# A planner's cost table with other figures for TensorE's products and GpSimd's powers (two-layer encoder, one core)

## The chip, the core and the metric

The kernel runs on one core of one Trainium2 chip. Five engines take part, each with its own instruction queue, which it works off in order: TensorE (PE; its weight loads are listed apart as PEld), ScalarE (ACT), VectorE (DVE), GpSimd (POOL) and SyncE (SP), which in this kernel issues every DMA. An instruction that waits for another engine holds up everything behind it in its own queue. The metric is the device time of one execution in microseconds (us); the time of a kernel is the median of its runs.

## The reference

The reference computes two layers of an encoder over one sequence of 256 tokens with 1024 features, all in float32. Each layer has an attention sublayer and a feed-forward sublayer:

```python
def mixer_sublayer(x, ...):
    proj = rms_norm(x, n1) @ w_in_l                      # 1024 -> 2560
    qa, ka, va, qd, kd, vd, qc, kc, vc = jnp.split(proj, cuts, axis=-1)
    out_a = neighbourhood_attention(...)                 # 4 heads, with a bias table
    out_d = dilated_window_attention(...)                # 6 heads, partial rotary
    out_c = gqa_block_attention(...)                     # 6 query heads on 2 key heads, axial rotary
    mix = jnp.concatenate([rms_norm(out_a, ...), rms_norm(out_d, ...), rms_norm(out_c, ...)], axis=-1)
    return x + mix @ w_out_l                             # 1024 -> 1024

def channel_sublayer(x, n2, w_gu, cw, cb, w_dn):
    g, u = jnp.split(rms_norm(x, n2) @ w_gu, 2, axis=-1) # 1024 -> 2 x 2816
    g = depthwise_conv_centred(g, cw, cb)                # three taps along the sequence
    return x + (jax.nn.gelu(g, approximate=False) * u) @ w_dn
```

Queries and keys are normed per head ahead of the scores.

## The kernel before

**Products.** A float32 product is made of three: each operand is split into a rounded high part and the rest, and `mm3` adds high × high, high × low and low × high into one PSUM bank. Weights come from HBM in units of up to 1 MB, into a ring of four raw buffers. ACT copies each unit into its high part (`wp_hi`), DVE subtracts to get the low part (`wp_lo`), in pieces of 512 columns; there are two buffers of each. Activations that are multiplied are transposed on TensorE, and ACT and DVE write high and low part (`act_hT`, `act_mixT_hi`, `act_mixT_lo`, `act_ch`, `act_cl`). PSUM has eight banks: four for accumulations of the projections (`psa_a`) and four for everything else (`psw_w`: scores, transposes, weighed values, the feed-forward's first products).

**Stages of a layer.** First come the input projections, in seven column groups (`projections`). The attention of 16 heads follows as a chain: scores on TensorE, maximum and exponential on DVE and ACT (`softens`), transposes on TensorE (`turn`), weighing with the values on TensorE (`weigh`), norm per group (`group_rstd`: squares on POOL, sums through products with ones on TensorE, a power on POOL). Between the steps of this chain the recording code puts filler: the rest of the projections and four of the six blocks of the output projection (class `Weave`; it counts the filler with a constant of its own, 2.4 columns per ns, which does not change). Then come the last two output blocks; `split_T(halves(0))` and `split_T(halves(1))`, which transpose the two halves of the new x into `act_hT`; and `mean_squares`, whose power on POOL gives `small_rx`. I call this place the feed-forward's head. The feed-forward part runs over 11 steps: a gate and an up block (`half_up`: per 128 rows of depth one product of 512 columns, high weight times high and low activations side by side, and one of 256, low weight times high), the convolution, the GELU, and a down block (`down`, products of 512 columns).

**The neighbourhood's bias table.** For each layer POOL copies a small table (`act_nab<-act_few`), SP writes it to HBM and reads it back along the diagonals (`na_repeat`, `na_diagonals`), and POOL adds a mask to it in three instructions (`act_nab<-act_nab,const_na`).

**Order of the work.** Nothing is issued while it is recorded. `Plan.add` notes each of the 5,580 operations with what it must wait for, and with a time from `cost()`. Then `Plan.order` simulates the five engines: again and again it takes, among all operations whose inputs are made, the one that can start first by its own clock; where two can start at the same time, the lower rank goes first. The rank is the place in the recording, plus a shift that the `later()` blocks give (weight splits 50, transposes of weights of attention 100, mixing 100, preparation of heads 30). A handover between engines costs a fixed time from a table (`HANDOVER`, for example 197 ns from TensorE to ACT); a buffer goes to its next user 170 ns after the last use. `Plan.emit` then issues the operations in that order, so the table decides on the order in each queue, and on the buffers, but not on what is computed. Since one line (345) issues everything, the profile shows one line for all instructions, and one reads it by the tiles' names.

In the simulation the start of an operation is

```python
at = max(o.at, free[e])      # inputs made, engine free; then the buffer's time
if at is not None and (best is None or (at, o.rank) < best[:2]):
    best = (at, o.rank, i)
```

Of the kernel before, what the change touches and what calls it, by code (L numbers as in the profile page):

```python
# [12 lines left out]
F32R = mybir.dt.float32r  # L13
# [202 lines left out]
class Plan:  # L216
# [15 lines left out]
    def add(self, engine, method, args, kw):  # L232
# [11 lines left out]
        if method == "matmul" and not kw["start"]:  # L244
            ins.append(args[0])
        o.ns, o.size = cost(engine.name, method, args, kw, ins)
        o.before, o.after, o.first, o.tiles = set(), [], [], []
        for v in ins + outs:
# [99 lines left out]
def cost(engine, method, args, kw, ins):  # L348

    out = args[0]  # L350
    if method == "dma_start":
        w = out if isinstance(out, View) else args[1]
        small = min(out.shape[-1], args[1].shape[-1]) < 128
        return 50, 4 * math.prod(w.shape) * (2 if small else 1)
    n = out.width()
    psum = any(v.tile.pool.psum for v in ins)
    if engine == "PE":
        if method == "transpose":
            return 110, 0
        n = args[2].width()  # L360
        if args[1].dtype == F32:
            return 108, 0
        return n / (2.4 if args[1].dtype == F32R else 1.2) + 2.5, 0
    if engine == "ACT":
        extra = 93 * sum(isinstance(kw.get(k), View) for k in ("scale", "bias")) + 90 * ("accum_out" in kw)
        return 0.833 * n + (47 if psum else 94) + extra, 0
    if engine == "DVE":
        if method in ("reduce_sum", "reduce_max"):
            n = args[1].width()
        per = 1.04  # L370
        if method in ("tensor_copy", "tensor_scalar_mul") and not psum:
            per = 0.52
        if method == "tensor_tensor_reduce":
            per = 1.3
        return per * n + (130 if method == "scalar_tensor_tensor" or method == "tensor_scalar_mul" and n > 16 else 70), 0
    if method == "memset":
        return 40 + 0.9 * n, 0
    if method == "tensor_copy":
        return 3.4 * n, 0
    if kw.get("op") == ALU.pow:  # L380
        return 300 + 165 * n, 0
    return 2.2 * n + 160, 0


# [958 lines left out]
```

## Time and profile before

| what | value |
| --- | --- |
| runs of the kernel | 631.75, 631.51, 630.89 us; median 631.51 |
| the profiled execution | 632.02 us |
| its span (first to last instruction) | 630.2 us |
| granted TensorE clock | 1.00 |
| TensorE busy | 616.0 us, 98% of the span |
| VectorE, ScalarE, GpSimd busy | 499.0 us (79%), 436.4 (69%), 90.6 (14%) |
| HBM traffic | 102.5 MB read, 1.5 MB written, 165 GB/s over the span |

The profile is taken from one execution. In its tables a row names the engine, the operation, and the tiles as output<-inputs; "x64" is a count. In a timeline the first two columns are start and duration in us, and brackets at the end hold the idle time of the engine before the row and what released it. The ends of products are modelled: the next product usually starts before the listed end of the one before, so the pace is read from starts, or from the length of a gapless run divided by its count. Layer 0's attention lies at about 16 to 128 us, its feed-forward part at 131 to 321; layer 1's attention at 322 to 436, and its feed-forward part at 438 to 626.

### The profile page before, as it was taken

To read this page: it belongs to the slowest core of one execution; us is meant where nothing else is said; L and a number is where in the kernel's file an instruction comes from. 1 tells how busy PE (TensorE), PEld (TensorE's weight loads), DVE (VectorE), ACT (ScalarE), POOL (GpSimd) and SP (SyncE) were. 2 spreads that over 40 slices of the span, in tenths; PEclk is the share of its full clock that TensorE was granted. 3 is DMA by queue.
4 is the path that set the end of the run, shared out by engine and by line. 5 is a ranking of instruction groups with operands and counts; after the bars stand their busy time and mean duration, and the time that the engine had idled before them with its cause. 6 is when DMAs were issued, how large, how long until landed. Compare 5 with 4: busy or idle time off the path is not lost.

```text
span 630.2 us, 9713 instructions
## 1 busy us (share of the span) xinstructions
PE 616.0 (98%) x3400; PEld 534.0 (85%) x3400; DVE 499.0 (79%) x1038; ACT 436.4 (69%) x1076; POOL 90.6 (14%) x139
## 2 busy tenths in 40 slices
PE   8998999999999999999999999999999999999997
PEld 6997888877888888888899989787888888888885
DVE  4799989899777777777877898988887777777775
ACT  6787998786665556556678989888756655666551
POOL 5755231350000000000013210311000000000000
PEclk9999999999999999999999999999999999999999
DMA  7894313486555655565434732134556555555511
GB/s 247 284 275 133 125 43 101 133 213 206 192 201 200 200 180 176 181 200 185 148 111 162 248 101 84 35 118 153 201 200 201 195 174 174 194 200 185 172 44 67
DMA packets 81408, 104.65 MB, mean 166 GB/s; under 512 B 9528, under 2 KB 69016, under 8 KB 81360
## 3 DMA queue, kind: packets, MB, share of 16 engines
q1 hardware_dynamic: 81360, 104.04, 51.1%
q8 instruction: 26, 0.43, 0.3%
q14 instruction: 22, 0.18, 0.1%
HBM read 102.54 MB, written 1.49 MB: 165 GB/s over the span
## 4 chain that ended last, share of the span: by engine, by line
PE 90%; DVE 5%; ACT 2%; POOL 1%; issue 1%; DMA 1%; SPq 0%; ACTq 0%; POOLq 0%
PE psw_w L345 48%; PE psa_a L345 41%; DVE wp_lo L345 1%; ACT act_s2k L345 1%; DVE act_s2k L345 1%; DVE act_z L345 1%; POOL small_rstd L345 1%; DMA const_x<-in_x_dram 1%; ACT wp_hi L345 1%; DVE small_mx L345 0%; ACT act_hT L345 0%; DVE small_ss L345 0%; DVE act_hT L345 0%; DVE act_cl L345 0%; SPq L345 0%
## 5 line engine op out<-in xcount | busy, mean ns | idle before, releaser
L345 DVE TENSOR_TENSOR wp_lo<-wp_raw,wp_hi 128x512 fp32r<-128x512 f32 (+2 forms) x348 | 250.7, 749 | 50.6 <-ACT wp_hi L345 48.8
L345 PE MATMUL psw_w<-act_hT,wp_hi 128*128 128x512 f32 x704 | 248.4, 394 | 3.6 <-DVE act_hT L345 3.6
L345 ACT CAST wp_hi<-wp_raw 128x512 fp32r<-128x512 f32 (+2 forms) x348 | 212.8, 659 | 26.9 <-PE psw_w L345 15.6
L345 PE MATMUL psw_w<-act_hT,wp_lo 128*128 128x256 f32 x704 | 198.3, 283 | 0.0
L345 PEld LDWEIGHTS psw_w<-act_hT,wp_hi 128*128 128x128 f32 x704 | 131.9, 188 | 34.6 <-DVE act_hT L345 4.7
L345 PEld LDWEIGHTS psw_w<-act_hT,wp_lo 128*128 128x128 f32 x704 | 132.3, 188 | 1.2
L345 PE MATMUL psa_a<-wp_hi,act_hT 128*128 128x384 f32 (+2 forms) x448 | 114.4, 335 | 0.0
L345 ACT COPY act_s2k<-psw_w 128x256 f32<-128x256 f32 x88 | 32.4, 372 | 81.4 <-PE psw_w L345 81.4
L345 PEld LDWEIGHTS psa_a<-wp_hi,act_hT 128*128 128x128 f32 x448 | 79.0, 189 | 2.5 <-DVE act_hT L345 0.2
L345 PE MATMUL psa_a<-wp_lo,act_hT 128*128 128x384 f32 (+2 forms) x224 | 75.2, 336 | 0.5 <-DVE wp_lo L345 0.5
L345 PE MATMUL psa_a<-wp_hi,act_ch 128*128 128x512 f32 x176 | 69.6, 395 | 0.2 <-ACT act_ch L345 0.2
L345 PE MATMUL psa_a<-wp_lo,act_ch 128*128 128x512 f32 x176 | 69.5, 395 | 0.0
L345 PE MATMUL psa_a<-wp_hi,act_cl 128*128 128x512 f32 x176 | 66.2, 395 | 0.3 <-DVE act_cl L345 0.3
L345 DVE TENSOR_TENSOR act_s2k<-psw_w,act_s2k 128x256 f32<-128x256 f32 x88 | 36.9, 423 | 31.2 <-ACT act_s2k L345 30.5
L345 PEld LDWEIGHTS psa_a<-wp_lo,act_hT 128*128 128x128 f32 x224 | 42.5, 190 | 3.2 <-DVE wp_lo L345 1.8
L345 PEld LDWEIGHTS psa_a<-wp_hi,act_cl 128*128 128x128 f32 x176 | 33.2, 188 | 8.5 <-DVE act_cl L345 0.8
L345 PEld LDWEIGHTS psa_a<-wp_hi,act_ch 128*128 128x128 f32 x176 | 33.1, 188 | 8.2 <-ACT act_ch L345 0.6
L345 PEld LDWEIGHTS psa_a<-wp_lo,act_ch 128*128 128x128 f32 x176 | 33.2, 189 | 6.8
L345 DVE SCALAR_TENSOR_TENSOR act_s2k<-act_s2k,act_cw,act_s2k 128x255 f32<-128x255 f32 x88 | 36.8, 480 | 1.4 <-ACT act_s2k L345 1.3
L345 ACT ACTIVATE act_s2k<-act_s2k,act_cw 128x256 f32<-128x256 f32 x44 | 24.1, 595 | 14.0 <-DVE act_s2k L345 14.0
L345 POOL TENSOR_TENSOR small_rstd<-small_ms,const_mh 128x6 f32<-128x6 f32 (+2 forms) x26 | 31.3, 1202 | 2.2
L345 POOL TENSOR_TENSOR small_s1x<-small_ssx 128x2 f32<-128x2 f32 x4 | 2.3, 582 | 200.5 <-ACT act_s2k L345 200.5
(112 smaller groups left out, 830.9 us busy)
## 6 DMA issues: line engine op xcount, KB each, us to landing
wp_raw<-in_w_gate_up_dram SPq DMA_DIRECT2D x44, 1024.0 KB, 5.1
wp_raw<-in_w_down_dram SPq DMA_DIRECT2D x22, 1024.0 KB, 4.8
wp_raw<-in_w_in_dram SPq DMA_DIRECT2D x14, 768.0 KB, 5.5
wp_raw<-in_w_in_dram SPq DMA_DIRECT2D x8, 1024.0 KB, 6.1
wp_raw<-in_w_out_dram SPq DMA_DIRECT2D x8, 768.0 KB
wp_raw<-in_w_out_dram SPq DMA_DIRECT2D x4, 512.0 KB, 3.8
act_nab<-dram_scr SPq DMA_DIRECT2D x4, 448.0 KB, 6.7
const_x<-in_x_dram SPq DMA_DIRECT2D x8, 128.0 KB, 3.6
```

The costliest lines, as they stand in the source:

```text
L345: getattr(o.engine.real, o.method)(*map(real, o.args), **{k: real(v) for k, v in o.kw.items()})
```

## The change

Two figures of `cost()` change. For a float32r product of n columns the time in the table was n/2.4 + 2.5 ns and is now 0.4405 n + 6.5 ns: for 512, 384 and 256 columns 215.8, 162.5 and 109.2 ns become 232.0, 175.7 and 119.3. The bfloat16 products that warm TensorE up at the start, 256 columns wide, go from 215.8 to 210 ns. A power on POOL of n columns goes from 300 + 165 n to 380 + 165 n ns. Transposes and the float32 products with ones keep their figures (110 and 108 ns).

```diff
@@ -360,7 +360,7 @@
         n = args[2].width()
         if args[1].dtype == F32:
             return 108, 0
-        return n / (2.4 if args[1].dtype == F32R else 1.2) + 2.5, 0
+        return (0.4405 * n + 6.5 if args[1].dtype == F32R else 210), 0
     if engine == "ACT":
         extra = 93 * sum(isinstance(kw.get(k), View) for k in ("scale", "bias")) + 90 * ("accum_out" in kw)
         return 0.833 * n + (47 if psum else 94) + extra, 0
@@ -378,7 +378,7 @@
     if method == "tensor_copy":
         return 3.4 * n, 0
     if kw.get("op") == ALU.pow:
-        return 300 + 165 * n, 0
+        return 380 + 165 * n, 0
     return 2.2 * n + 160, 0
```

The operations are the same 5,580 with the same operands; each engine gets them in another order, and some take another buffer of the same ring.

## The prediction

> **What bounds the kernel now.** I read the page's first lines first, then the table of busy time by stretch, the list of what TensorE waited for, and the timeline at each wait.
>
> ```profile
> span 630.2 us, 9713 instructions
> PE 616.0 (98%) x3400; PEld 534.0 (85%) x3400; DVE 499.0 (79%) x1038; ACT 436.4 (69%) x1076; POOL 90.6 (14%) x139
> PE 90%; DVE 5%; ACT 2%; POOL 1%; issue 1%; DMA 1%; SPq 0%; ACTq 0%; POOLq 0%
> ```
>
> TensorE is busy for 98% of the span and carries 90% of the chain that ended last. The change leaves its instructions as they are, so what can be won or lost is TensorE's idle time. Where it lies, by stretch (columns: stretch, its length, then busy time and count of PE, PEld, DVE, ACT, POOL, the granted clock, DMA):
>
> ```profile
> 24.00:32.00 8.00, 7.46 (x44) 6.67 (x43) 7.24 (x16) 5.79 (x32) 7.49 (x10) 1.00 0.67 226
> 48.00:60.00 12.00, 10.33 (x72) 9.31 (x71) 11.94 (x34) 9.30 (x34) 8.13 (x11) 1.00 0.41 131
> 85.00:92.00 7.00, 6.58 (x43) 5.61 (x42) 6.63 (x19) 6.13 (x19) 4.55 (x6) 1.00 0.13 48
> 120.00:130.00 10.00, 9.32 (x54) 7.60 (x53) 8.63 (x16) 6.06 (x14) 2.15 (x3) 1.00 0.49 150
> 130.00:140.00 10.00, 8.80 (x52) 7.28 (x51) 9.75 (x17) 8.45 (x22) 5.78 (x6) 1.00 1.19 269
> 150.00:155.00 5.00, 4.44 (x20) 3.15 (x19) 4.99 (x9) 3.61 (x9) 0.00 (x0) 1.00 0.36 108
> 155.00:300.00 145.00, 145.00 (x763) 123.98 (x762) 108.28 (x184) 86.39 (x157) 0.00 (x0) 1.00 0.57 191
> 390.00:400.00 10.00, 9.08 (x60) 7.76 (x60) 8.21 (x22) 9.11 (x28) 4.54 (x5) 1.00 0.18 53
> 436.00:447.00 11.00, 8.63 (x54) 7.29 (x53) 9.61 (x19) 8.61 (x23) 1.85 (x3) 1.00 0.36 113
> ```
>
> TensorE idles 0.54 us in 24–32, 1.67 in 48–60, and in the six later stretches 0.42, 0.68, 1.20, 0.56, 0.92 and 2.37, together 6.15. The feed-forward part (155–300) has none. The waits, summed over the run (us, times, longest):
>
> ```profile
> PE psw_w L345 <- DVE act_hT L345: 3.6, 4, 1.2
> PE psw_w L345 <- DVE act_cl L345: 1.3, 2, 0.9
> PE psw_w L345 <- POOL const_warm L345: 1.0, 1, 1.0
> PE psw_w L345 <- DMA const_x<-in_x_dram: 0.9, 1, 0.9
> ...
> PE psa_a L345 <- ACT act_ch L345: 0.2, 1, 0.2
> ```
>
> The 11 rows of this list add up to 10.2 us in 15 waits. The largest is act_hT, the normed input of the feed-forward part, at its head in both layers.
>
> **The change, part by part.** Two lines of the table change: the pace of a product and the time of a power.
>
> ```profile
> 157.59 11.22 PE psw_w L345 x64
> 168.81 5.58 PE psa_a L345 x24
> L345 POOL TENSOR_TENSOR small_rstd<-small_ms,const_mh 128x6 f32<-128x6 f32 x12 | 17.3, 1444 | 1.0
> L345 POOL TENSOR_TENSOR small_rstd<-small_ms,const_mh 128x2 f32<-128x2 f32 x10 | 7.4, 736 | 0.8
> ```
>
> The chain's 24 products of 512 columns took 5.58/24 = 0.2325 us each; 32 pairs (512 and 256 columns) 11.22/32 = 0.351. The old table says 0.2158 and 0.325, the new one 0.2320 and 0.3513: the old is 7% fast, the new fits. Powers of width 6 and 2 took 1.444 and 0.736 us; old 1.290 and 0.630, new 1.370 and 0.710.
>
> [...]
>
> What this does to the order: of 3,388 TensorE operations 1,047 stand elsewhere, nearly all in the two attention stages (59–139 and 362–446 us), by up to 40 places; 326 of ACT's, 402 of DVE's, 10 of POOL's, 8 of SP's. With slower products the planner sees chain products (scores, transposes, weighings, ones-sums) ready after fewer filler products, so they come earlier, and filler (projections, output projection) is left for later. At the feed-forward's head:
>
> ```profile
> 433.96 1.03 POOL L345 TENSOR_TENSOR small_rstd<-small_ms,const_mh 128x2 f32<-128x2 f32 x1
> 435.02 2.73 DVE L345 SCALAR_TENSOR_TENSOR const_x<-psa_a,small_rstd,const_x 128x512 f32<-128x512 f32 x4 [0.60 <-POOL small_rstd L345]
> 436.20 0.38 PE L345 MATMUL psw_w<-const_ident,const_x 128*128 128x128 f32 x2
> 438.59 0.50 PE L345 MATMUL psw_w<-act_hT,wp_hi 128*128 128x512 f32 x1 [1.12 <-DVE act_hT L345]
> 136.40 0.50 PE L345 MATMUL psw_w<-act_hT,wp_hi 128*128 128x512 f32 x1 [1.01 <-DVE act_hT L345]
> 136.74 0.28 PE L345 MATMUL psw_w<-act_hT,wp_lo 128*128 128x256 f32 x1
> 443.77 0.51 PE L345 MATMUL psw_w<-act_hT,wp_hi 128*128 128x512 f32 x1 [1.25 <-DVE act_hT L345]
> ```
>
> - Price of a stall: its idle, plus a restart (136.40 to 136.74 is 0.34 where 0.23 is the pace, so 0.11), plus what the modelled end hides; I take 0.25 on top. The six later stretches hold about 9 stalls: 6.15 + 9 × 0.25 = 8.4 us at stake.
> - First block of layer 1's head: eight output products now stand behind the last transposes, 8 × 0.2325 = 1.86 us of cover against 1.12 + 0.25. The stall goes. Layer 0 the same. Late next: the transposes, placed ten earlier (10 × 0.23 = 2.3 us); their const_x starts only when POOL's power ends (434.99), so the new wait is 0 to 2.3. The ones-sums that feed the power also moved eleven places ahead, so I put it with the new waits below.
> - Second blocks: four transposes now stand ahead of six products that stood ahead of them (two of 512 columns, four of 256: 2 × 0.2325 + 4 × 0.1185 = 0.94 us of cover) against 1.25 and 1.01. About 0.9 each goes.
> - 85–92, 120–130, 150–155, 390–400: chain products come ahead of DVE's and ACT's weight casts, and products whose data are there take the idle. I count 85% of all 8.4 as gone: −7.2, between −4.2 (half) and −8.4.
> - New waits: every product placed earlier can meet data that are not there. No row shows these; the nearest are the present waits, 10.2 us in 15, 0.68 each. Following the new order with present durations I find four likely places (the scores of the compressed heads near 75 us and their twins in layer 1, the transposes above), so 4 × 0.6 = +2.4, between 0 and 12 × 0.68 = 8.2.
> - Feed-forward steady state: six products of each down step swap hi and lo; DVE and ACT have the same queues and are 75% and 60% busy in 155–300. 0; without that cover 0.11 for each of some twenty steps.
> - SP: conv loads and the neighbourhood table's write go one place ahead of a raw weight load. Raw loads are four deep; 0.
> - Startup: one more warm-up and a transpose behind the x transfer. +0.2, between −0.9 and +0.9, the wait for const_x.
> - 24–32: the weight cast goes ahead of act_z, −0.6. But 48–60 does not end by TensorE's order:
>
> ```profile
> 51.98 0.55 DVE L345 TENSOR_TENSOR act_z<-psa_a,small_rstd 128x384 f32<-128x384 f32 x1
> 52.40 1.32 POOL L345 TENSOR_TENSOR small_rstd<-small_ms,const_mh 128x6 f32<-128x6 f32 x1
> 53.69 1.41 POOL L345 TENSOR_TENSOR act_nab<-act_nab,const_na 128x576 f32<-128x576 f32 x1
> 53.87 1.65 DVE L345 TENSOR_TENSOR act_z<-act_z,act_ccq 128x384 f32<-128x384 f32 x1
> 54.22 0.33 PE L345 MATMUL psw_w<-const_ident,act_s2k 128*128 128x128 f32 x1 [0.86 <-ACT act_s2k L345]
> 56.44 0.68 DVE L345 TENSOR_TENSOR wp_lo<-wp_raw,wp_hi 128x512 fp32r<-128x512 f32 x1
> 56.57 0.55 PE L345 MATMUL psw_w<-const_ident,act_z 128*128 128x128 f32 x3 [0.81 <-DVE act_z L345]
> ```
>
> Beside the neighbourhood add on POOL (53.69), DVE's act_z, two SBUF tensors in, took 1.65 us where its like took 0.55: 1.1 us lost to the add. The change moves that add ahead of the power at 52.40 and moves the cast of 56.44 forward into the softmax chain: the cast would meet the add and take 0.7 + 1.1, and the transposes of 54.22 come up to 1.8 late. Their products behind (0.5 us) and the second stall absorb most: TensorE is 0.4 later at 57 us than before, between 0 and 1.4, and the 0.6 won at 24–32 is gone by then, since this chain ends by DVE and POOL.
>
> [...]
>
> Sum: −7.2 + 2.4 + 0.2 + 0.4 = −4.2 on the profiled 632.0 us (span 630.2 and 1.8 around it). That execution is 0.5 above the median 631.5, so 627.3.
>
> **Rivals.**
> 1. The covers hold and no new waits come: −7.2 + 0.6 = −6.6, 624.9; at the best all 8.4 and the 0.6, 622.5. For it: new filler of 1.86 us exceeds each wait it covers. Against it: 15 places already wait in an order that saw the same handovers.
> 2. The change does not do what it says: stalls only move, since DVE is 11.94 of 12 us busy in 48–60 and 9.75 of 10 in 130–140, so what bounds there is DVE. 631.5, ±1.3.
> 3. Slower: the chain's products stand too early. Place: the attention stages, where 838 of the moves lie. Each that meets missing data costs 0.68. With −7.2 + 0.6 otherwise, it is even at 6.6/0.68 = 10 such waits, and at 13 the time is 631.5 + 2.2 = 633.7. For it: 40 places are 7 us of filler (40 × 0.351/2), far more than the longest present wait of 1.2, so products were moved past much more than they needed. Against it: the new pace is the measured one, and its plan for TensorE is nearer the truth.
> 4. Most of it lost again on POOL, in layer 0's head:
>
> ```profile
> 127.54 1.58 SPq L345 DMA_DIRECT2D act_nab<-dram_scr x2
> 134.04 1.62 POOL L345 TENSOR_TENSOR small_s1x<-small_ssx 128x2 f32<-128x2 f32 x1 [6.70 <-ACT act_s2k L345]
> 136.70 5.11 POOL L345 TENSOR_TENSOR act_nab<-act_nab,const_na 128x576 f32<-128x576 f32 x3
> 139.29 0.38 PE L345 MATMUL psw_w<-const_ident,small_rx 128*128 128x128 f32 x2
> ```
>
> One of the adds at 136.70 now stands ahead of small_s1x at 134.04. If its data land where they do now (reads issued at 127.54 to 129.1, adds from 136.70), small_s1x starts at 136.7 + 1.7 and the transposes of small_rx, 2.5 us behind the power now, are late by 4.4 − 2.5 = 1.9, and DVE's casts beside the add lose 1.1: 627.3 + 1.9 + 1.1 = 630.3, and with the full loss at 52 us (1.4 for 0.4) 631.3. It decides from a landing later than 134.0 − 1.7 = 132.3. Against it: the write of that table now goes ahead of a raw load that waits for its buffer, so the reads come earlier.
>
> **How the numbers follow.** Forecast (625 to 630): 0.48. Rival 1: 0.14. Rival 2: 0.11, of it 0.01 slower. Rival 3: 0.19. Rival 4: 0.08, of it 0.03 faster, 0.03 the same and 0.02 slower. Within 0.2% (1.3 us) is about what measurement can't tell from no change. Faster: 0.48 + 0.14 + 0.03 = 0.65; same: 0.10 + 0.03 = 0.13; slower: 0.19 + 0.01 + 0.02 = 0.22. The range reaches from just under rival 1's best, 622, to 633.5, inside rival 3; outside is 0.05 below and 0.12 above. The likeliest's own range is 625 to 630.
>
> **What would show it.** Right: no wait above 0.4 us for act_hT in 130–140 and 436–447; 390–400 above 9.7 us busy; 48–60 no better than now. Wrong: new waits of TensorE for act_s2k, act_z or const_x in 60–130 or 362–436 adding up to more than 6 us; small_rx late behind act_nab; a slower pace in 155–300.

## The result and the profile after

The changed kernel takes 635.45 us (median of 4 runs, 634.29 to 635.92) against 631.36 for the kernel before (median of 4, 630.89 to 631.75): a ratio of 1.0059, with a 95% interval of 1.0046 to 1.0072. It is slower by 0.6%. The forecast was 627.3, with a range that ended at 633.5. The profiled execution took 635.28 us, 633.5 of it span, so it can be set against the 632.02 and 630.2 of before: 3.3 us more.

The page of the changed kernel, its span, TensorE's busy time, the granted clock in 40 slices, and the chain that ended last:

```profile
span 633.5 us, 9708 instructions
PE 620.4 (98%) x3400; PEld 533.6 (84%) x3400; DVE 498.9 (79%) x1038; ACT 435.0 (69%) x1076; POOL 92.2 (15%) x139
PEclk9998999998999999999999999999999999999999
PE 80%; DVE 7%; ACT 4%; DMA 4%; POOL 2%; issue 2%; SPq 1%; POOLq 0%; DVEq 0%; ACTq 0%
```

The work is the same, yet TensorE is "busy" for 620.4 us instead of 616.0, and two slices of the clock show an 8 where the kernel before had 9 throughout. TensorE's share of the chain fell from 90% to 80%. The table of busy time by stretch (the last three columns are the granted clock, the DMA share and GB/s):

```profile
24.00:32.00 8.00, 7.90 (x46) 7.13 (x45) 7.73 (x15) 7.38 (x38) 7.29 (x9) 1.00 0.85 284
48.00:60.00 12.00, 9.37 (x59) 8.75 (x58) 11.01 (x35) 7.91 (x22) 6.95 (x11) 0.86 0.43 146
85.00:92.00 7.00, 6.99 (x55) 6.51 (x54) 6.82 (x19) 6.91 (x21) 5.23 (x6) 1.00 0.04 13
120.00:130.00 10.00, 9.91 (x53) 8.07 (x52) 7.63 (x14) 4.06 (x10) 2.49 (x3) 1.00 1.09 282
130.00:140.00 10.00, 9.68 (x53) 7.69 (x53) 9.23 (x16) 8.87 (x23) 4.90 (x6) 1.00 1.00 254
150.00:155.00 5.00, 3.24 (x14) 2.18 (x13) 4.97 (x8) 4.75 (x9) 0.00 (x0) 0.89 0.53 202
160.00:300.00 140.00, 140.00 (x736) 119.74 (x735) 103.23 (x173) 82.54 (x149) 0.00 (x0) 1.00 0.56 188
390.00:400.00 10.00, 9.79 (x73) 9.05 (x72) 8.47 (x25) 8.94 (x27) 4.20 (x5) 1.00 0.22 81
436.00:447.00 11.00, 10.58 (x55) 8.08 (x55) 8.86 (x17) 8.52 (x22) 3.38 (x5) 1.00 0.37 121
```

Most of the gains that were forecast are there: the idle time in 85–92 went from 0.42 to 0.01, in 120–130 from 0.68 to 0.09, in 130–140 from 1.20 to 0.32, in 390–400 from 0.92 to 0.21, in 436–447 from 2.37 to 0.42. Two stretches went the other way, 48–60 (1.67 to 2.63 idle) and 150–155 (0.56 to 1.76), and both show a clock below 1. The waits say the same, with act_hT down from 3.6 us to 0.6:

```profile
PE psw_w L345 <- ACT act_s2k L345: 3.0, 2, 2.6
...
PE psa_a L345 <- DVE act_cl L345: 1.2, 2, 1.0
...
PE psa_a L345 <- ACT act_ch L345: 0.8, 1, 0.8
PE psw_w L345 <- DVE act_hT L345: 0.6, 2, 0.3
```

Idle time leaves out short gaps and slow products, since the ends of products are modelled. I therefore also added up, over all neighbouring products, the distance of their starts less the pace of that form (0.2324 us for 512 columns, 0.1753 for 384, 0.1195 for 256, 0.1095 for transposes and for the warm-up products). This excess, in us, for the kernel before, the changed one, and two runs that are told of below:

| stretch | before | changed | both stages repaired | new pace in layer 1's head alone |
| --- | --- | --- | --- | --- |
| 0–50 | 6.75 | 4.81 | 5.74 | 6.68 |
| 50–60, softmax stage | 2.15 | 4.40 | 2.30 | 2.20 |
| 60–130 | 2.46 | 2.52 | 2.65 | 2.45 |
| 130–150, layer 0's head | 1.69 | 1.82 | 1.84 | 1.68 |
| 150–160, first down block | 1.07 | 3.84 | 1.15 | 1.10 |
| 320–470, layer 1 up to the first down block | 4.83 | 4.84 | 4.81 | 4.04 |

The loss is in two places of 10 us, 2.25 and 2.77 us; the long attention stages and layer 1 came out even to about 0.1 us, although the long waits in them went. The first two rows belong together: the changed profile is 1.9 us ahead at 50 us, 1.6 of it since the first 10 us, and loses that lead at 50–60. Over 0–60 it is only 0.3 us behind (9.2 against 8.9), and with both stages repaired 0.9 ahead (8.0).

**The softmax stage.** Timelines of the changed kernel on POOL, DVE, ACT and TensorE; the first adds start 1.5 us earlier here than in the kernel before (44.30 against 45.82):

```profile
44.30 3.79 POOL L345 TENSOR_TENSOR act_nab<-act_nab,const_na 128x576 f32<-128x576 f32 x2 [5.57 <-DMA act_nab<-dram_scr]
50.19 1.42 POOL L345 TENSOR_TENSOR act_nab<-act_nab,const_na 128x576 f32<-128x576 f32 x1
```
```profile
49.36 0.08 DVE L345 DVE_READ_ACCUMULATOR2_ANT small_mx<- 128x1 f32 x1
50.24 0.56 DVE L345 TENSOR_TENSOR act_z<-psa_a,small_rstd 128x384 f32<-128x384 f32 x1 [0.79 <-POOL small_rstd L345]
50.72 0.92 DVE L345 TENSOR_SCALAR small_nm<-small_mx 128x2 f32<-128x2 f32 x1
```
```profile
51.67 0.51 ACT L345 ACTIVATE act_s2k<-act_s2k,small_nm 128x256 f32<-128x256 f32 x1 [2.76 <-DVE small_nm L345]
```
```profile
54.39 0.33 PE L345 MATMUL psw_w<-const_ident,act_s2k 128*128 128x128 f32 x1 [2.63 <-ACT act_s2k L345]
```

The row maximum is there at 49.44, but small_nm, which the exponential needs, now stands behind act_z in DVE's queue. act_z waits for a power on POOL, and that power waits behind two neighbourhood adds whose table came by DMA. small_nm then runs beside the third add, which the change moved ahead of the second power, and takes 0.92 us where the kernel before needed 0.17. The kernel before, on POOL, DVE and ACT:

```profile
45.82 3.48 POOL L345 TENSOR_TENSOR act_nab<-act_nab,const_na 128x576 f32<-128x576 f32 x2 [6.14 <-DMA act_nab<-dram_scr]
51.90 0.17 DVE L345 TENSOR_SCALAR small_nm<-small_mx 128x2 f32<-128x2 f32 x1
52.11 0.51 ACT L345 ACTIVATE act_s2k<-act_s2k,small_nm 128x256 f32<-128x256 f32 x1 [1.85 <-DVE small_nm L345]
```

So the exponential starts at 51.67, only 0.44 us before that of the old kernel. The reciprocal of its sum (small_rs) then stands behind a weight subtraction on DVE that the change moved ahead, and comes at 53.64 instead of 53.46, so the transposes start at 54.39, 0.17 us later than the old kernel's. TensorE was 2.0 us further on in its queue by then: it had nothing left and stood for 2.63 us.

**The first down block.** ACT in the changed kernel, then ACT in the kernel before:

```profile
147.26 1.28 ACT L345 ACT_TABLE_LOAD   x1 [1.73 <-DVE act_s2k L345]
148.55 0.63 ACT L345 ACTIVATE act_s2k<-act_s2k 128x512 f32<-128x512 f32 x1
149.09 0.63 ACT L345 COPY act_s2k<-psw_w 128x256 f32<-128x256 f32 x2
149.61 2.01 ACT L345 CAST wp_hi<-wp_raw 128x1024 fp32r<-128x1024 f32 x2
151.51 0.62 ACT L345 CAST act_ch<-act_s2k 128x512 fp32r<-128x512 f32 x1
```
```profile
144.92 1.03 ACT L345 CAST wp_hi<-wp_raw 128x1024 fp32r<-128x1024 f32 x1
146.75 1.28 ACT L345 ACT_TABLE_LOAD   x1 [0.80 <-DVE act_s2k L345]
...
150.49 0.62 ACT L345 CAST act_ch<-act_s2k 128x512 fp32r<-128x512 f32 x1
```

Before, one of the two casts of the down block's weights ran at 144.92, while ACT waited for the convolution. Now the GELU stands ahead of it. The GELU is not ready, it needs DVE's last tap and a table load of 1.28 us, so ACT stands idle and both casts come after it, between the GELU and act_ch. On DVE the two subtractions that follow them (2.35 us) now go ahead of act_cl, and TensorE waits twice:

```profile
150.88 2.35 DVE L345 TENSOR_TENSOR wp_lo<-wp_raw,wp_hi 128x1024 fp32r<-128x1024 f32 x2
153.15 0.69 DVE L345 TENSOR_TENSOR act_cl<-act_s2k,act_ch 128x512 fp32r<-128x512 f32 x1
```
```profile
153.89 0.79 PE L345 MATMUL psa_a<-wp_hi,act_cl 128*128 128x512 f32 x1 [0.98 <-DVE act_cl L345]
154.48 0.63 PE L345 MATMUL psa_a<-wp_hi,act_ch 128*128 128x512 f32 x1
154.91 0.63 PE L345 MATMUL psa_a<-wp_lo,act_ch 128*128 128x512 f32 x1
...
157.04 0.53 PE L345 MATMUL psa_a<-wp_hi,act_ch 128*128 128x512 f32 x1
```

**The clock.** The last rows show a second loss. From 154.48 to 157.04 the products follow each other at 0.43 us, not 0.2325, six of them. The granted clock, third from the right in these rows, is halved there until 157.3, then the old pace is back; the same happens behind the stall that ended at 54.39, up to 58.3:

```profile
54.95:58.35 3.40, 3.40 (x18) 3.30 (x16) 3.23 (x11) 2.88 (x9) 1.39 (x5) 0.50 0.35 92
153.95:157.30 3.35, 3.35 (x8) 2.68 (x9) 3.35 (x7) 1.77 (x4) 0.00 (x0) 0.50 0.88 295
```

About 3.4 us of products at 0.43 instead of 0.2325 us cost some 1.6 us each time. The first fall came behind the stall of 2.63 us, the second behind the pair of 0.77 and 0.98 us.

### The profile page after: what moved, and what is told of

It reads as the page before. It is cut to its first block, busy times and chain, and to the rows that moved or that the text cites. A ratio compares the mean times of both kernels' runs of the same rounds, so it can differ in the third digit from the quotient of the medians.

```text
span 633.5 us, 9708 instructions
## 1 busy us (share of the span) xinstructions
PE 620.4 (98%) x3400; PEld 533.6 (84%) x3400; DVE 498.9 (79%) x1038; ACT 435.0 (69%) x1076; POOL 92.2 (15%) x139
## 4 chain that ended last, share of the span: by engine, by line
PE 80%; DVE 7%; ACT 4%; DMA 4%; POOL 2%; issue 2%; SPq 1%; POOLq 0%; DVEq 0%; ACTq 0%
PE psw_w L345 44%; PE psa_a L345 36%; DVE wp_lo L345 3%; ACT act_s2k L345 1%; DMA act_nab<-dram_scr 1%; DVE act_s2k L345 1%; POOL small_rstd L345 1%; DVE const_x L345 1%; DMA dram_scr<-act_nab 1%; ACT wp_hi L345 1%; DMA wp_raw<-in_w_gate_up_dram 1%; SPq L345 1%; DMA wp_raw<-in_w_in_dram 1%; ACT L345 1%; POOL act_nab L345 1%
## 5 line engine op out<-in xcount | busy, mean ns | idle before, releaser
L345 PE MATMUL psa_a<-wp_hi,act_cl 128*128 128x512 f32 x176 | 70.1, 400 | 1.2 <-DVE act_cl L345 1.2
```

The source lines that it names most:

```text
L345: getattr(o.engine.real, o.method)(*map(real, o.args), **{k: real(v) for k, v in o.kw.items()})
```

## The experiments

My theory A: the loss sits in these two stages, where the order put a chain operation ahead of work that was ready, or ready work ahead of the chain, and the clock made each worse. The rivals: B, the loss is spread over new waits in the attention stages; C, it comes from the powers; D, the clock fell for another reason; E, the softmax stage is bound by the neighbourhood table's DMA whatever DVE's order is; F, the first down block is late because of casts that take longer beside the neighbourhood adds. In the edits below numbers are operations in the order of recording, and (a, b) puts operation a directly ahead of b in the issue order; nothing else changes unless it is said. All kernels compute the whole result.

Each run was compared with runs of the kernel before on the same chip, whose median was 631.39 to 631.53 us, and 632.27 in one group (the second direction and the first run with the new pace late in layer 1 and the adds moved).

### One line at a time, and one layer

The pace alone:

```diff
-        return 380 + 165 * n, 0
+        return 300 + 165 * n, 0
```

> The table with the new pace of products, but the old time of powers. Theory A (the loss sits at two places of layer 0, the softmax stage near 52 us and the first down block near 152 us, where the new pace put the chain's operations in another order, and each place is made worse by a fall of the granted clock): the pace line alone brings at least one of the two places back, so 633 to 636 us with the clock below 1. Rival C (the loss comes from the longer powers, which moved the neighbourhood adds ahead of the power): 629 to 631.5 us, clock 1.0.

Measured 634.65 us, ratio 1.0046 (1.0031 to 1.0061), clock 0.996. The pow line alone, in the kernel before:

> The old pace of products and the new time of powers. Theory A: nothing much, 630.5 to 632 us at a clock of 1.0. Rival C: most of the 4 us, 634 to 636.

631.48, ratio 1.000 (0.9989 to 1.0012). So rival C is out: the pace brings most of the loss, and the powers alone bring none. But the pace alone brings only one of the two places. Against the kernel before, its profile has 2.0 us more excess in 50–60, at a mean clock of 0.996, and 0.6 less at the first down block; the rest of its loss, 1.5 us in 60–130 and 0.7 in 130–150, lies in waits of the attention stage and the head, as rival B has it. The first down block's new order needs both lines. Layer 1 alone:

```diff
+        NEW[0] = i >= 2835        # in Plan.add, ahead of cost(); cost() takes the new figures if NEW[0]
```

> Both new figures, but only for the operations recorded from layer 1's first transposes on; layer 0 keeps the old table. Theory A: the excess of TensorE's starts over its pace is 4.88 us before and 4.82 after in layer 1, so the time of the kernel before, 631.4 within 0.6, clock 1.0. Rival B (the loss is spread over new waits of the chain's products in the attention stages of both layers, my third rival of the prediction): half of the loss, 633.4.

631.61, ratio 0.9994 (0.9984 to 1.0004), as theory A had it. Its excess in 320–470 is 4.83 us, the same as before, so rival B is out for layer 1.

### Filling the stalls: is it the clock?

```diff
+FILLS = {542: (24, 542), 1558: (8, 1558), 1560: (10, 1564)}   # ahead of this operation: count, whose bank
...
+                if i in FILLS:      # n warm-up products of 256 columns into the bank of operation j
```

> The changed kernel with idle-filling products of ones (128x256 bfloat16, into a bank that the next product overwrites) ahead of the three longest stalls of layer 0: 24 ahead of the transposes at 54.4 us, 8 and 10 ahead of the products at 152.2 and 153.9. The waits stay. Theory A: the granted clock stays at 1.0 and the slow products behind the stalls are gone (about 1.4 us at 56 to 58 and 1.75 us at 154 to 157.5), so 632.0 to 632.8 us. If the clock falls for another reason (rival D): 635.3 or a little more, clock 0.993 as now.

633.83 us, ratio 1.0035; no execution of five had a mean clock below 0.999, where all four of the changed kernel had 0.993 to 0.997. The two stretches of its profile:

```profile
56.00:60.00 4.00, 4.00 (x23) 3.37 (x22) 4.00 (x13) 3.99 (x10) 1.39 (x5) 1.00 0.66 198
150.00:157.00 7.00, 7.00 (x42) 5.63 (x41) 7.00 (x12) 5.19 (x11) 0.00 (x0) 1.00 0.59 201
```

With TensorE busy in both stretches its clock stayed at 1.00 there, so rival D is out and the falls follow from the stalls. The gain of 1.6 us was half of what I expected. Part of the rest went into something new: the transposes of small_rx waited 1.5 us for POOL at 139, since one neighbourhood add now stands ahead of small_s1x and its data came late; the excess in 130–150 is 1.0 us above that of the changed kernel. That is the prediction's fourth rival, which the changed kernel's own profile escaped (its power ended at 138.27, and TensorE came to these transposes at 139.10).

### Undoing the two stages in the new order

The softmax stage as before, on DVE (small_nm, 528, ahead of act_z, 498; the casts 594 and 596 back), TensorE and POOL (the third add, 733, behind the second power):

```diff
+MOVES = ((526, 594), (528, 498), (534, 499), (531, 503), (535, 503), (536, 504), (513, 504), (596, 598),
+         (543, 548), (544, 548), (545, 548), (640, 548), (641, 548), (733, 3240))
```

> The changed kernel's order, but in the stage at 46 to 58 us the old order on three queues: VectorE's row maximum and small_nm ahead of act_z, the weight casts behind act_z; the third neighbourhood add behind the power on GpSimd; the four transposes of act_s2k ahead of those of act_z on TensorE. Theory A: the stall of 2.8 us at 54.4 shrinks to about 1.2, the clock no longer falls there (0.87 and 0.71 in 52 to 60), the excess in 50 to 60 goes from 4.4 to about 2.5: 633.5, between 633 and 634.5. If the stage is bound by the neighbourhood table's DMA and adds whatever the order on VectorE is (rival E): the stall stays above 2 us and the time at 635.

633.77, ratio 1.0047 (1.0029 to 1.0065). The stall of 2.63 us is gone; a wait of 1.2 us for act_z is left, the excess in 50–60 is 2.34. Rival E is out as the cause of the long stall; the 2.3 us that are left are those of the kernel before, and they go when the adds do (below). The first down block:

```diff
+MOVES = ((1501, 1451), (1502, 1494))    # cast ahead of the GELU, its subtraction ahead of the joins
```

> The changed kernel's order, but ScalarE's cast of the first down block's second piece goes ahead of the first GELU again, and VectorE's subtraction for it ahead of the joins of the up block. Theory A: act_ch 0.5 us and act_cl 1.0 us earlier, the stalls of 0.94 and 1.14 at 152 to 154 about halved, no fall of the clock there (0.78 in 150 to 157), so 2.0 to 2.8 us less: 632.6 to 633.4. If the late operands come from the casts that the neighbourhood adds lock out at 138 to 142 (rival F): the stall moves little, 635.

632.38, ratio 1.0018 (1.0009 to 1.0028): a little better than expected. The excess in 150–160 fell from 3.84 to 1.14. Of these 2.7 us about 1.6 are the clock: the profile of the run with the softmax stage repaired has the two waits at this block unchanged (0.8 and 1.0 us) and no fall (a clock of 1.00 in 150–160), and 2.27 us. Both:

> Both repairs together. Theory A: the two gains add up, 630.5 to 631.5 us at a clock of 1.0, the kernel before within its noise or just below it. Rival B (spread waits): 633 or more.

632.24, ratio 1.0014 (1.0005 to 1.0024). The two gains don't add up; some 0.9 us over the kernel before are left. In its profile, the fastest of its ten executions at 631.6 us, the excess of all stretches but the first 50 us is within 0.2 of before, so these 0.9 sit in no stage that I can name.

### The same two swaps in the old order

To see whether they alone make the loss, I put them into the kernel before: the cast behind the GELU and its subtractions ahead of act_cl; then the softmax stage's new order; then both.

```diff
+MOVES = ((1501, 1503), (1537, 1550), (1502, 1538), (1538, 1551))                            # first down block
+MOVES = ((594, 526), (498, 528), (596, 499), (534, 531), (503, 531), (504, 536), (733, 511),  # softmax stage
+         (542, 638), (543, 640), (544, 640), (545, 640), (548, 543), (549, 640), (550, 640))
```

> The kernel before with only the first down block's order of the changed kernel: ScalarE's cast of the second piece behind the first GELU, VectorE's two subtractions for it ahead of act_cl. Theory A: act_ch about 0.5 us and act_cl 1.2 us later than now, the stalls there grow from 0.41 and 0.48 to about 0.9 and 1.1, and in part of the runs the clock falls (0.003 of the mean clock, 1.8 us): 632.5 to 634. If the swap does harm only with the rest of the new order: 631.4.

633.05, ratio 1.0010 (0.9994 to 1.0026): unclear by its interval, but the waits grew as expected, from 0.2 and 0.3 us to

```profile
PE psa_a L345 <- ACT act_ch L345: 0.7, 1, 0.7
PE psa_a L345 <- DVE act_cl L345: 0.5, 1, 0.5
```

> The kernel before with only the softmax stage's order of the changed kernel: small_nm behind act_z and the weight casts ahead of it on VectorE, the third neighbourhood add ahead of the second power on GpSimd, and TensorE's transposes in the new order. Theory A: the transposes of act_s2k come 1.5 to 1.8 us later than 54.2, one stall of 2.3 to 2.9 us in place of 1.0 and 1.0, the clock falls in most runs: 632.5 to 634. If the stage is bound by the table's DMA alone: 631.4.

633.22, ratio 1.0022 (1.0005 to 1.0038), with one wait for act_s2k of 2.8 us in place of two of 0.9 and 0.8, and 8 of 10 executions below a mean clock of 0.999.

> The kernel before with both. Theory A: the sum of the two, 634 to 636, with the clock below 1 in most runs, the time of the changed kernel with one six-hundredth of its moves. If there is a third cause of the size of the two: below 633.5.

634.58, ratio 1.0043 (1.0027 to 1.0058), 5 of 6 executions below 0.999 (beside it the kernel before, on this chip, 10 of 21). Eighteen hand-made moves of single operations, about one for each hundred operations that the prediction counts as moved (not one for each six hundred, as expected above), cost 0.43% of the 0.59%. So theory A holds for about three quarters by the medians, though the intervals allow from under a half to all of it; the rest, 0.1 to 0.2%, agrees with what was left after both repairs, and with rival B in so far as the rest of the new order gains nothing.

### Taking the adds away

In both stages DVE's work or a power stands behind the neighbourhood adds on POOL. First I moved layer 0's three adds to near 70 us, and then to 57 us:

```diff
+         (731, 3404), (732, 3404), (733, 3404)    # both repairs, and adds near 70 us
```

> Both repairs, and the three neighbourhood adds of layer 0 on GpSimd moved from 44 to 51 us to behind the powers of the next head group near 70 us. Theory A with the table's DMA as the anchor of the softmax stage: powers come 3 us earlier, VectorE's casts at 44 to 49 us are not locked out (2.4 us), the stall at 54 goes: 629 to 630. If the adds do no harm there: as the run with both repairs; if they harm as much near 70 us: no more than 0.5 less.

635.29, ratio 1.0058 (1.0043 to 1.0073): 3 us above the run with both repairs. The timeline shows why:

```profile
66.21 4.25 DVE L345 TENSOR_TENSOR act_sw<-act_z,act_sck 128x32 f32<-128x32 f32 x4
66.24 4.17 POOL L345 TENSOR_TENSOR act_nab<-act_nab,const_na 128x576 f32<-128x576 f32 x3
...
71.73 0.56 DVE L345 TENSOR_TENSOR act_sw<-act_z,act_sck 128x32 f32<-128x32 f32 x4
```

Four operations of 32 columns on DVE, two SBUF tensors in, took 4.25 us beside the adds, as long as the adds ran, and TensorE waited 3.1 us; four of the same form took 0.56 at 71.73, where no add ran. The softmax stage itself had no wait left.

```diff
+         (731, 656), (732, 656), (733, 656)       # both repairs, and adds behind the rotary tables
```

> The run with both repairs, and layer 0's three neighbourhood adds moved on GpSimd from 44 to 54 us to behind the rotary tables near 58 us, ahead of the next powers, where VectorE is busy for 2.8 of 4 us. If the softmax stage was bound by the table's DMA and by casts locked out beside the adds: no wait above 0.4 us in 48 to 60, 2.3 us of excess gone there, up to 1.5 new at 58 to 66: 630.0 to 631.3. If the adds cost the same wherever they run (as near 70 us, 3.2 us in one stall): 632 or more.

634.50, ratio 1.0042 (1.0031 to 1.0054). A weight subtraction and act_z beside the adds took 1.90 and 1.80 us, where their like took 0.65 and 0.55 at 52.8 to 54.6 in the same profile, TensorE waited 1.1 and 1.8 us at 59 and 64, and 7 of 10 executions had a mean clock of 0.997 or less. So at both places the adds lengthened what DVE had to do then, and in this attention stage DVE has little idle time (busy 11.94 of 12 us in 48–60 and 22.14 of 25 in 60–85 in the run with both repairs). Then layer 1's adds, which run in layer 0's head, by reading their table back behind two more weight loads:

```diff
+         (1894, 1549), (1895, 1549), (3485, 1549), (3486, 1549), (3487, 1549)    # both repairs, and these
```

> The run with both repairs, and layer 1's table read back behind two more weight loads, so that its three adds on GpSimd run in the feed-forward part after 150 us instead of at 135 to 142. Rival F of the cast run (the late operands of the first down block come from casts locked out by these adds): the stalls of 0.62 at 141, 0.41 and 0.52 at 151 go, and small_rx is never late: 630.5 to 631.3. If the adds only took idle time there, or if they stall the feed-forward part as much: 632.2.

630.39, ratio 0.9977 (0.9963 to 0.9991), 1.9 us below the run with both repairs. The adds now wait for their data until the feed-forward part,

```profile
149.76 5.11 POOL L345 TENSOR_TENSOR act_nab<-act_nab,const_na 128x576 f32<-128x576 f32 x3 [14.77 <-DMA act_nab<-dram_scr]
```

and in 130–160 one wait of 0.3 us is left of these four (the run with both repairs):

```profile
PE psw_w L345 <- DVE wp_lo L345: 0.5, 1, 0.5
PE psa_a L345 <- DVE act_cl L345: 0.4, 1, 0.4
PE psw_w L345 <- DVE act_hT L345: 0.3, 1, 0.3
PE psa_a L345 <- ACT act_ch L345: 0.2, 1, 0.2
```

The same is seen in three weight subtractions of the head on DVE, 4.34 us in the run with both repairs, beside two of the adds, and 1.89 in this run, without them:

```profile
136.82 4.34 DVE L345 TENSOR_TENSOR wp_lo<-wp_raw,wp_hi 128x512 fp32r<-128x512 f32 x3
```
```profile
136.29 1.89 DVE L345 TENSOR_TENSOR wp_lo<-wp_raw,wp_hi 128x512 fp32r<-128x512 f32 x3
```

The two weight loads that the edit lets pass were issued only 1.4 and 0.4 us earlier here (125.14 and 133.91, against 126.49 and 134.32), so they don't explain it. So rival F was right beside theory A: the order and the subtractions beside the adds both made the first down block late. Both moves of adds together, on the new order and then on the old one:

> Both moves of adds on top of both repairs. If the two gains add: 628.5 to 630, faster than the kernel before by 0.2 to 0.5%. If either collides with something: no better than the better one of the two.

630.85, ratio 0.9991 (0.9981 to 1.0002): no better than with layer 1's adds alone moved, with the same waits of 1.1 and 1.8 us.

> The kernel before, old table and old order, with only the two moves of adds. If the adds on GpSimd are what bounds the two stages whatever the table is: 628.5 to 630, as the run with everything on the new table or better, since the new table gained nothing elsewhere. If the new table's chain-first order is needed to use the room: 631 or more.

630.15, ratio 0.9974 (0.9962 to 0.9986). The old order with the adds moved is no worse than the new one with adds moved and repairs.

### The part of the new order that pays

```diff
+        NEW[0] = i >= 3900        # new figures from the last third of layer 1's attention on
```

> The kernel before, with the new figures only for operations recorded from the last third of layer 1's attention on; layer 0 and the adds stay. If the head's new order pays by itself: 1.0 to 1.8 us below the kernel before, and the waits for act_hT in 425 to 447 fall from 2.4 us to below 0.6. If it is paid back by waits further up: within 0.5 of the kernel before.

630.61, ratio 0.9985 (0.9975 to 0.9996): 0.8 us, just under what was expected. The wait for act_hT at the head fell from 2.4 us to

```profile
PE psw_w L346 <- DVE act_hT L346: 0.3, 1, 0.3
```

With the two moves of adds:

> The kernel before with the two moves of adds, and with the new pace only for operations recorded from the last third of layer 1's attention on, so that its feed-forward's head gets the new order (eight output products behind the transposes). If the gain there stands by itself: 0.9 to 1.5 us below the run with the two moves, 628.7 to 629.3. If it is paid back by small waits as in the whole change: 630.2.

628.66, ratio 0.9946 (0.9929 to 0.9962), 1.5 us below the run with the moves alone by the medians, at the far end of what was expected. And with layer 0's head as well:

```diff
+        NEW[0] = 1180 <= i < 1440 or i >= 3900
+MOVES = ((731, 656), (732, 656), (733, 656), (1894, 1549), (1895, 1549), (3485, 1549), (3486, 1549), (3487, 1549))
```

> The two moves of adds, and the new figures for both feed-forward heads (operations from layer 0's last third of attention to its first up block, and in layer 1 as in the run beside it). If both heads pay: 1.0 to 1.8 us for each and 1.2 for the moves, 3.2 to 4.8 us below the kernel before. If layer 0's head pays nothing: 2.2 to 3.0 below.

628.20, ratio 0.9943 (0.9923 to 0.9963), the best of the study, though not clear of the run with layer 1's head alone, 3.2 us below the kernel before and 7.2 below the changed one by their medians; its 120–130 has 1.5 us less excess than that run, its 130–150 and 60–120 together 1.2 more, so layer 0's head gave back most of what it gained. In its softmax stage and in layer 1's head there is hardly anything left to win:

```profile
48.00:60.00 12.00, 12.00 (x85) 10.98 (x84) 11.96 (x34) 10.12 (x32) 8.04 (x11) 1.00 0.35 121
436.00:447.00 11.00, 10.67 (x63) 8.78 (x62) 10.76 (x23) 8.73 (x20) 1.91 (x3) 1.00 0.58 187
```

## Why the prediction was wrong

Set against the terms of the forecast, the excess by stretch says which steps failed. Up to 60 us, +0.6 was forecast and +0.3 came. In 60–150 and 320–470, −3.9 was forecast (−7.2 without the 0.9 of the first down block, and +2.4 of new waits), and +0.2 came. At the first down block, −0.9 was forecast, and +2.8 came. So two steps failed: the new waits, put at 2.4 us, were some 6, and the stalls of the first down block, counted as gone, grew, for the order's sake and the clock's.

- **What bounds the kernel** (TensorE, and its idle places): right. The gains and losses lie in the stretches that were named. All three signs that were to show it right came (act_hT at 0.3 us, 390–400 at 9.79, 48–60 no better), and none of those against it but the 2.3 us of halved clock behind 155: the signs watched the stalls that were to go, not the places that then lost.
- **The price of the table** (old 7% fast, new one fitting): right as a measurement. That a truer figure gives a better order, on which the argument against rival 3 rested, was not. The rest of the table stayed as it was: it knows nothing of the GELU's table load (1.28 us) or of what DVE loses beside the adds (4.25 us for 0.56 at 66 us). That an order with less slack in front of the chain meets such errors sooner is my reading; no run changed those figures.
- **Later stalls, −7.2**: the stalls in 85–140 and 390–447, 6.8 us by starts, shrank by 5.9 with their stages otherwise repaired. The two at the first down block, which the step counted as gone with the words that chain products come ahead of the weight casts, grew: 0.9 became 2.1, because the chain's operation there, the GELU, was not ready, and the cast behind it was. The step looked at what stands ahead, not at what then stands behind a wait.
- **New waits, +2.4**: mis-sized. Since 60–150 and 320–470 came out even, 5.9 us of gain met about 6 us of new waits, inside the bound of 8.2 that was given. They are many and small: of the gaps between 0.09 and 0.23 us there were 15 in 60–160 and 320–470 before and 35 with both stages repaired, of those between 0.23 and 0.4 there were 1 and 7. The four likely places were among the new waits, with 0.25 to 0.34 each.
- **24–32 and 48–60, +0.4 less 0.6**: that a lead is gone by 60 us, since this chain ends by DVE and POOL, was right, and at 60 us TensorE was 0.3 later, close to the forecast. Its parts were not: what met the moved add was small_nm, put behind act_z, and not the subtraction of 56.44 (it took its usual 0.68); and there is luck in the sum, since a lead of 1.9 us, more than forecast, hid most of a loss of 2.25, about 1.4 of it by the clock (2.96 us of excess in 50–60 where the kernel before had this stage's new order and no fall came, 4.40 in the changed kernel).
- **The clock**: not in the prediction at all. The rows before showed 1.00 in every stretch, with stalls up to 1.25 us, and I priced stalls by their length alone. One profile could not show more: of the kernel before, 24 of the 99 executions beside the runs above had a mean clock below 0.999. The two falls are about 3 of the 5.0 us that the two stages lost.
- **Startup, +0.2**: the first 50 us had 1.9 us less excess in the changed profile. It is 4.8 to 6.3 in profiles with the new start and 6.5 to 7.0 in most with the old one, but 5.5 and 5.7 in two, so I leave open how much of this is the order.
- **Rivals**: rival 3's waits came and ate the gain, just short of the 6.6 us from which they would decide alone. Rival 4 did not decide in the changed kernel, but cost a wait of 1.5 us as soon as the stalls ahead of it were filled. Rival 2 had named what bounds 48–60 and 130–140, DVE, and was nearest for everything but the two stages.
- **The adds beside DVE**: the prediction counted a loss of 1.1 us for DVE at 52 us, and again in rival 4. Moving them, from the run with both repairs, made the time longer by as much as 3.1 us and shorter by 1.9.

## What to carry to other kernels

In a list scheduler, one corrected figure among many wrong ones shifts every tie: look at each place where an operation that the trace shows not to be ready now stands in an in-order queue ahead of one that is, and keep what pays by region, as with the heads here. A stall can have a second price when TensorE's clock falls behind it, here some 1.6 us each time in the changed kernel; with the stalls filled with dummy products all five executions kept 0.999 or more. An engine that is 14% busy can still set the order: put its operations where the engine that is slower beside them has slack, here in the feed-forward part (DVE 75% busy in 155–300), where layer 1's adds cost 1.9 us less.

## What the runs showed of the hardware

- In the changed kernel's profile the granted clock was halved from 54.94 us, behind a TensorE stall of 2.63 us, and from 153.92, behind two of 0.77 and 0.98 us within 2.5 us. Both halved stretches last 3.413 us in the clock's record, and they begin 98.99 us apart. The profile with the new figures in layer 1 alone, layer 0 planned as before, had a mean clock of 0.996. The clock did not fall each time: with the stall at 54 us in place and the first down block repaired, 3 of 10 executions had a mean clock of 0.997 and took 633.6 us at the median, the other seven, at 1.0, 632.2. Behind the stalls of 0.8 and 1.0 us at 152 it fell in the changed kernel's profile and not in that with the softmax stage repaired (1.00 in 150–160). What decides it, no run here shows. With the adds moved, alone and with the new pace late in layer 1 (48–60 busy 12.00 of 12 us in the profile of the latter), all 10 executions had 0.999 or more; with the new pace in both heads (12.00 of 12 too), 4 of 5.
- Operations on DVE took longer beside a GpSimd add of 576 columns. Four of 32 columns with two SBUF inputs took 4.25 us beside three adds of 4.17, against 0.56 for four of the same form with no add beside them, and the last ended 0.05 us behind the last add. One with a single input and 2 columns, small_nm, took 0.92 us instead of 0.17, until 0.03 us behind the add.
- The GELU's table load took 1.28 us on ACT and started 0.08 us behind the last tap on DVE that the GELU needs, in both profiles (146.75 and 147.26), so it sat on the path and not in the idle time of 0.80 and 1.73 us ahead of it.
